# A hybrid-attention layer stack in FP32 by split products on one Trainium2 core: two chunks of the down projection as seven block products

## The chip, the cores and the metric

The kernel runs on one core of a Trainium2 chip. The metric is the device time of one execution in microseconds (us). The kernel before has a median of 1004.43 us over three runs (1003.47 to 1004.53). All inputs and the output are float32.

## The reference

The model has two layers on 256 tokens of width 1024. Each layer is a feed-forward network (ffa), a mixer (two kinds of attention) and a second feed-forward network (ffb); each adds its result to x. The change touches the feed-forward networks alone:

```python
def swiglu(x, w_gate, w_up, w_down):
    return (jax.nn.silu(x @ w_gate) * (x @ w_up)) @ w_down
...
    for l in range(DEPTH):
        x = x + 0.5 * swiglu(rms_norm(x, ffa_norm[l]), ffa_w_gate[l], ffa_w_up[l], ffa_w_down[l])
        x = x + hybrid_mixer(rms_norm(x, mix_norm[l]), w_in[l],
        ...
        x = x + 0.5 * swiglu(rms_norm(x, ffb_norm[l]), ffb_w_gate[l], ffb_w_up[l], ffb_w_down[l])
    return rms_norm(x, final_norm)
```

So four feed-forward networks run in a program. In each, w_gate and w_up are 1024 x 2816 and w_down is 2816 x 1024.

## The kernel before, in words

**Split products.** A float32 matrix is split into two float32r parts, high (`whi`, `xhi`, `hhi`) and low (`wlo`, `xlo`, `hlo`). A product of two such matrices is three matmuls, high by high, high by low and low by high, which `prod3` (L316 to L324) issues at L321, L322 and L323. For weights, ScalarE copies 128 x 1024 elements to the high part (L302) and VectorE subtracts that from the raw tile to get the low part (L281). One unit of weights is 1 MB (2048 elements on each partition) and takes two such pairs.

**A feed-forward network.** The 2816 hidden columns are five chunks of 512 and a half chunk of 256; the 256 tokens are two tiles t of 128. For chunks 0, 2, 4 and 5, gate and up are plain products. For chunks 1 and 3, gate and up together are a 2 x 2 block product (two token tiles by two halves of the input width, times those two halves by gate and up) and go by seven block products instead of eight, named 1 to 7. Four of them need sums of blocks of x on the left, which VectorE makes and which are split into the tiles named `fnhi`, `fnlo`, `fohi`, `folo`. The weights' sums are made by DMA: the tile that holds one block, when it is split, is added to in place by a second transfer from HBM (`accum_op` add, on the queue of GpSimd, L261), and is then split again. Products 1, 5, 6 and 4 share one tile in such a chain, 3 and 7 another, and 2 has its own. The result h = silu(gate) * up is turned by TensorE (L549) and split into `hhi` (L554) and `hlo` (L556).

**The down projection.** h (22 blocks k of 128 rows) is multiplied by w_down, as 11 units of two k each (`down`, from L699). Four accumulators of one PSUM bank each (token tile t by column half c, tag `acc`) collect all 22 k. One unit is 2 x 2 x 2 x 3 = 24 matmuls of 512 columns. The last two units (`TAIL`) go accumulator by accumulator, so that `close` (L720) can add 0.5 times a finished accumulator to x (L723) while the next one runs.

**What sets the order.** The program is written by generators that a small planner (`Flow`) steps in the order of its own clock and cost table, so the order of each engine's instructions is fixed when it is built. `loader` fetches the raw tiles in the order in which units are made, on the queue of SyncE (L247), with 5 raw tiles. `adder` issues the adding transfers on GpSimd's queue, in their order, each when the split before it in its chain is over. `splitter` splits the units in their order, with 6 pairs of split halves, that is, 3 units; a pair comes free when the last matmul that reads it is over. The list `PLANS` orders the products of gate and up: "g0" is the gate of chunk 0, "41" is product 4 of chunk 1.

The two lines around which the stage turns:

```python
                    prod(pd[t, c], hs, t, k, u, i, slice(c * 512, (c + 1) * 512), k == 0, k == 21)
...
            nc.vector.scalar_tensor_tensor(x[:, t, sl], pd[t, c], 0.5, x[:, t, sl],
```

Of the kernel before, what the change touches and what calls it, by code (L numbers as in the profile page):

```python
# [44 lines left out]
    "g0 u0 11 g2 51 21 31 u2 61 71 13 g4 41 53 23 33 u4 63 73 h5 43".split(),) * 3  # L45
AC = 0.1
# [86 lines left out]
def hybrid_kernel(ctx, tc, x_in, ffa_norm, ffa_w_gate, ffa_w_up, ffa_w_down, mix_norm, w_in,  # L133
# [310 lines left out]
    def ffn_units(wg, wu, wd, plan, first):  # L444
# [6 lines left out]
        def block(c, m, kh):  # L451
            return cols((wg, wu)[m], c * 512, 512, kh)
# [12 lines left out]
        for z in plan:  # L465
            kind, c = z[0], int(z[1:])
            if kind in "gu":
# [3 lines left out]
            elif kind == "h":  # L471
                for kh in range(2):
                    us[z, kh] = order([cols(wg, 2560, 256, kh), cols(wu, 2560, 256, kh)], 4, 512)
            elif kind in "1564":
                step(("x", c), c, kind, *{"1": (0, 0), "5": (1, 0), "6": (1, 1), "4": (0, 1)}[kind], kind == "4")
            elif kind in "37":
                step(("y", c), c, kind, *{"3": (1, 1), "7": (1, 0)}[kind], z == [q for q in plan if q[0] in "37" and q[1:] == z[1:]][-1])
            else:
                step(("z", c), c, kind, 0, 1, True)
        for j in range(11):  # L480
            src = wd[j * 256:(j + 1) * 256].rearrange("(i p) n -> p i n", i=2)
            us["d", j] = order(src, 2, 1024)
        return us

    def ffn(us, nm, nxt, plan, last=False):
# [8 lines left out]
        def event(*k):  # L494
            return evs.setdefault(k, Event())
# [196 lines left out]
        if inner:  # L692
            fl.spawn(factors())
            fl.spawn(sums(), 1)
        for i, z in enumerate(plan):
            if z[0] in "1234567":
# [6 lines left out]

        def down(j, t, cs, free):
            u = us["d", j]
            yield ev[j // 2, t]
            for c in cs:
                if j == 0:
                    yield fl.get("acc")
                    pd[t, c] = bank("acc", 4)  # L710
                for i in range(2):
                    k = 2 * j + i
                    yield u.when(i)
                    prod(pd[t, c], hs, t, k, u, i, slice(c * 512, (c + 1) * 512), k == 0, k == 21)
# [4 lines left out]

        def close(t, c):  # L720
            sl = slice(c * 512, (c + 1) * 512)
            yield fl.clock + HOP
            nc.vector.scalar_tensor_tensor(x[:, t, sl], pd[t, c], 0.5, x[:, t, sl],  # L723
# [6 lines left out]
        for j in range(11 - TAIL):  # L730
            for t in range(T):
                yield from down(j, t, (0, 1), t == 1)
# [3 lines left out]
        for i, (t, c) in enumerate(ends):  # L736
            for j in range(11 - TAIL, 11):
                yield from down(j, t, (c,), i == 3)
# [913 lines left out]
```

## Time and profile before

| what | us or share |
|---|---|
| median of three runs | 1004.43 |
| the profiled execution, its own time | 1003.63 |
| its span, first to last instruction | 1001.8 |
| TensorE matmul busy | 989.3 (99%) |
| TensorE weight load busy | 826.5 (82%) |
| VectorE busy | 735.1 (73%) |
| ScalarE busy | 611.0 (61%) |
| granted TensorE clock, mean | 0.998 |

The busy times are those of the profile's page; a matmul's recorded end is modelled and lies behind the start of the next, so the share of TensorE is read together with its waits. The span is 1.8 us shorter than the execution's own time. The four down projections start at 131.7, 442.2, 623.4 and 934.1 us of the span and last about 61 us each. Line numbers in the rows are those of the kernel before.

### The profile page before, as it was taken

How to read it: one execution, taken by the hardware profiler on the slowest of the kernel's cores; microseconds unless marked ns; L12 is line 12 of the kernel's file. 1: busy time of each engine (PE TensorE's matmuls, PEld its weight loads, DVE VectorE, ACT ScalarE, POOL GpSimd, SP SyncE). 2: the span in 40 equal slices, each digit the busy share in tenths (PEclk: the TensorE clock that was granted, in tenths of full speed). 3: DMA queues.
4: the chain of work that ended last, by engine and by line, in shares of the span. 5: the costliest groups of instructions: out<-in, count | busy, mean ns of one | idle time of the engine just before them, and what ended most of it. 6: DMA issues, size and time to landing. Idle time of an engine off the chain costs nothing.

```text
span 1001.8 us, 14192 instructions
## 1 busy us (share of the span) xinstructions
PE 989.3 (99%) x5268; PEld 826.5 (82%) x5268; DVE 735.1 (73%) x1365; ACT 611.0 (61%) x1061; POOL 53.6 (5%) x61
## 2 busy tenths in 40 slices
PE   9999999999999999999999999999999999999997
PEld 7877888898987888888888888888988878888885
DVE  6889854587787978784488768447878789688544
ACT  7666553558785676653367566336687766665433
POOL 1021000100000011100001110001000001110000
PEclk9999999999999999999999999999999999999999
DMA  9899965363743799975548998553645238999611
GB/s 337 260 206 303 292 236 177 103 201 111 270 137 116 194 255 278 267 266 184 195 143 225 295 270 267 195 182 114 213 171 203 91 126 222 284 262 305 229 65 42
DMA packets 100981, 207.62 MB, mean 207 GB/s; under 512 B 3784, under 2 KB 23376, under 8 KB 100912
## 3 DMA queue, kind: packets, MB, share of 16 engines
q1 hardware_dynamic: 83072, 171.65, 49.2%
q0 software_dynamic: 17536, 34.54, 19.3%
q8 instruction: 41, 0.67, 0.3%
q10 hardware_dynamic: 304, 0.53, 0.1%
q14 instruction: 28, 0.23, 0.1%
HBM read 205.66 MB, written 1.05 MB: 206 GB/s over the span
## 4 chain that ended last, share of the span: by engine, by line
PE 93%; DMA 2%; DVE 2%; issue 1%; ACT 1%; POOL 0%; POOLq 0%
PE acc L321 19%; PE acc L323 18%; PE acc L322 18%; PE sb L322 7%; PE sb L323 7%; PE sb L321 7%; DMA raw<-in_ffa_w_up_dram 2%; PE acc L338 2%; PE acc L339 2%; PE acc L340 2%; PE acc L1079 2%; PE tb L549 2%; PE tb L1059 2%; PE tb L407 1%; DVE wlo L281 1%
## 5 line engine op out<-in xcount | busy, mean ns | idle before, releaser
L281 DVE TENSOR_TENSOR wlo<-raw,whi 128x1024 fp32r<-128x1024 f32 (+2 forms) x404 | 450.2, 1136 | 169.2 <-ACT whi L302 168.7
L302 ACT ACTIVATE whi<-raw 128x1024 fp32r<-128x1024 f32 (+2 forms) x404 | 388.0, 990 | 236.8 <-PE acc L323 99.2
L321 PE MATMUL acc<-whi,hhi 128*128 128x512 f32 x352 | 138.4, 393 | 0.0
L323 PE MATMUL acc<-whi,hlo 128*128 128x512 f32 x352 | 137.2, 390 | 0.0
L322 PE MATMUL acc<-wlo,hhi 128*128 128x512 f32 x352 | 137.0, 389 | 0.0
L321 PE MATMUL acc<-whi,xhi 128*128 128x512 f32 (+1 forms) x336 | 131.9, 392 | 0.0
L322 PE MATMUL acc<-wlo,xhi 128*128 128x512 f32 (+1 forms) x336 | 128.0, 381 | 0.0
L323 PE MATMUL acc<-whi,xlo 128*128 128x512 f32 (+1 forms) x336 | 127.9, 381 | 0.0
L322 PE MATMUL sb<-wlo,xhi 128*128 128x512 f32 x304 | 118.5, 390 | 0.8 <-DVE wlo L281 0.8
L321 PE MATMUL sb<-whi,xhi 128*128 128x512 f32 x304 | 119.3, 392 | 0.0
L323 PE MATMUL sb<-whi,xlo 128*128 128x512 f32 x304 | 118.5, 390 | 0.0
L323 PEld LDWEIGHTS acc<-whi,hlo 128*128 128x128 f32 x352 | 66.1, 188 | 14.0
L322 PEld LDWEIGHTS acc<-wlo,hhi 128*128 128x128 f32 x352 | 66.1, 188 | 13.5
L321 PEld LDWEIGHTS acc<-whi,hhi 128*128 128x128 f32 x352 | 66.1, 188 | 13.2
L323 PEld LDWEIGHTS acc<-whi,xlo 128*128 128x128 f32 x336 | 63.1, 188 | 12.2
L321 PEld LDWEIGHTS acc<-whi,xhi 128*128 128x128 f32 x336 | 63.4, 189 | 11.2 <-issue 0.7
L322 PEld LDWEIGHTS acc<-wlo,xhi 128*128 128x128 f32 x336 | 63.3, 188 | 10.5
L322 PEld LDWEIGHTS sb<-wlo,xhi 128*128 128x128 f32 x304 | 57.1, 188 | 12.8 <-DVE wlo L281 1.2
L323 PEld LDWEIGHTS sb<-whi,xlo 128*128 128x128 f32 x304 | 57.1, 188 | 12.0
L321 PEld LDWEIGHTS sb<-whi,xhi 128*128 128x128 f32 x304 | 57.1, 188 | 11.6
L338 PE MATMUL acc<-xhi,whi 128*128 128x256 f32 x192 | 56.5, 294 | 0.0
L339 PE MATMUL acc<-xlo,whi 128*128 128x256 f32 x192 | 54.2, 282 | 0.0
(230 smaller groups left out, 1431.2 us busy)
## 6 DMA issues: line engine op xcount, KB each, us to landing
raw<-in_ffa_w_down_dram SPq DMA_DIRECT2D x22, 1024.0 KB, 5.0
raw<-in_ffb_w_down_dram SPq DMA_DIRECT2D x22, 1024.0 KB, 5.0
raw<-in_w_in_dram SPq DMA_DIRECT2D x20, 1024.0 KB, 5.0
raw<-in_ffb_w_gate_dram SPq DMA_DIRECT2D x20, 1024.0 KB, 5.3
raw<-in_ffa_w_gate_dram SPq DMA_DIRECT2D x18, 1024.0 KB, 8.2
raw<-in_ffa_w_up_dram SPq DMA_DIRECT2D x16, 1024.0 KB, 7.3
raw<-in_ffb_w_up_dram SPq DMA_DIRECT2D x16, 1024.0 KB, 6.6
raw<-in_ffa_w_up_dram POOLq DMA_DIRECT2D x12, 1024.0 KB, 9.7
```

The source lines that it names most:

```text
L281: nc.vector.tensor_tensor(view(u, lo, i, True), source(u, i), view(u, hi.bitcast(F32), i, True), OP.subtract)
L302: nc.scalar.activation(view(u, u.halves[-1][0], i, True), source(u, i), AF.Copy)
L321: nc.tensor.matmul(ps, xh, wh, start=first, stop=False, skip_group_check=True)
L322: nc.tensor.matmul(ps, xh, wl, start=False, stop=False, skip_group_check=True)
L323: nc.tensor.matmul(ps, xl, wh, start=False, stop=last, skip_group_check=True)
L338: nc.tensor.matmul(ps, wh, xs[0][:, k], start=first and j == 0, stop=False, skip_group_check=True)
L339: nc.tensor.matmul(ps, wh, xs[1][:, k], start=False, stop=False, skip_group_check=True)
L340: nc.tensor.matmul(ps, wl, xs[0][:, k], start=False, stop=last, skip_group_check=True)
L407: nc.tensor.transpose(ps[:, i * n + (t - ts[0]) * 128:i * n + (t - ts[0] + 1) * 128], x[:, t, k * 128:(k + 1) * 128], ident)
L549: nc.tensor.transpose(ps[:, j * 128:(j + 1) * 128], h[:, j * 128:(j + 1) * 128], ident)
L1059: nc.tensor.transpose(ps[:, j * 128:(j + 1) * 128], pp[:, i * n + s_ * 128:i * n + (s_ + 1) * 128], ident)
L1079: nc.tensor.matmul(grp.o[u * 64:(u + 1) * 64, h // 2 * 128:(h // 2 + 1) * 128], val(s_), pT[:, j * 128:(j + 1) * 128], start=u not in grp. ...
```

## The change

For the chunks 0 and 2 (k = 0 to 3 and 8 to 11), the down projection is seen as a 2 x 2 block product: two token tiles by two chunks of h, times two chunks by two column halves of w_down. It is computed by seven block products of four k each. The other seven units (p2, p3, p6 to p10) stay as they were. `DOWN` gives the order: "5d" is product 5, "p8" is the old unit 8. Products 2, 3 and 4 add straight into three of the four accumulators. Products 1, 5, 6 and 7 go into banks with the tag `sb`, are combined by VectorE with tiles that ScalarE copied (`rest_d`), and are added to x by VectorE (`add_x`) before `close` adds the accumulators. Sums of blocks of h are made by VectorE (`sums_d`), from the moment at which the last product of gate and up, 43, is next (`AHEAD`), and are split into the same four buffers as the sums of x. The weights' sums are made as in gate and up: the chain 1d, 5d, 6d, 4d in one raw tile, 3d, 7d in a second, 2d alone.

```diff
@@ -43,6 +43,8 @@
 HOP = 0.3
 PLANS = ("g0 u0 g2 11 u2 51 21 31 13 61 71 g4 41 53 23 33 u4 63 73 h5 43".split(),) + (
     "g0 u0 11 g2 51 21 31 u2 61 71 13 g4 41 53 23 33 u4 63 73 h5 43".split(),) * 3
+DOWN = "1d p2 2d p8 5d p9 3d p3 6d p6 7d 4d p7 p10".split()
+AHEAD = 1
...
@@ -449,6 +451,9 @@
         chain = {}
 
         def block(c, m, kh):
+            if c == "d":
+                r = (0, 2)[kh] * 512
+                return wd[r:r + 512, m * 512:(m + 1) * 512].rearrange("(k p) n -> p k n", p=128)
             return cols((wg, wu)[m], c * 512, 512, kh)
 
         def step(key, c, p, m, kh, end):
@@ -462,9 +467,13 @@
             us[p, c] = Unit(r, done=end)
             chain[key] = (chain[key][0], us[p, c])
 
-        for z in plan:
-            kind, c = z[0], int(z[1:])
-            if kind in "gu":
+        for z in plan + DOWN:
+            kind = z[0]
+            c = "d" if z[1] == "d" else int(z[1:])
+            if kind == "p":
+                src = wd[c * 256:(c + 1) * 256].rearrange("(i p) n -> p i n", i=2)
+                us["d", c] = order(src, 2, 1024)
+            elif kind in "gu":
                 m = "gu".index(kind)
                 for kh in range(2):
                     us[z, kh] = order(block(c, m, kh), 4, 512, loads=4 if first and z == plan[0] else 1)
@@ -474,12 +483,9 @@
...
             elif kind in "37":
-                step(("y", c), c, kind, *{"3": (1, 1), "7": (1, 0)}[kind], z == [q for q in plan if q[0] in "37" and q[1:] == z[1:]][-1])
+                step(("y", c), c, kind, *{"3": (1, 1), "7": (1, 0)}[kind], z == [q for q in plan + DOWN if q[0] in "37" and q[1:] == z[1:]][-1])
             else:
                 step(("z", c), c, kind, 0, 1, True)
-        for j in range(11):
-            src = wd[j * 256:(j + 1) * 256].rearrange("(i p) n -> p i n", i=2)
-            us["d", j] = order(src, 2, 1024)
         return us
 
     def ffn(us, nm, nxt, plan, last=False):
@@ -692,7 +698,53 @@
         if inner:
             fl.spawn(factors())
             fl.spawn(sums(), 1)
+        dforms, dk = {}, {}
+
+        def sums_d():
+            for c in (0, 2):
+                for t in range(T):
+                    yield ev[c, t]
+            blocks = []
+            for t in range(T):
+                for c in (0, 2):
+                    yield fl.get("work")
+                    a = wk([128, 512], "a")
+                    h, l = (z[:, 4 * c:4 * c + 4, t * 128:(t + 1) * 128].bitcast(F32) for z in hs)
+                    nc.vector.tensor_tensor(a.rearrange("p (k c) -> p k c", k=4), h, l, OP.add)
+                    yield fl.dve(512)
+                    blocks.append(a)
+            a11, a12, a21, a22 = blocks
+            ho, lo = ([big.tile([128, 4, 256], F32R, name="f" + z, tag=z).rearrange(
+                "p a b -> p (a b)").rearrange("p (f n) -> p f n", f=2) for z in tags]
+                for tags in (("nhi", "ohi"), ("nlo", "olo")))
+            todo = iter((("5", 0, a22), ("6", 1, a11), ("3", 2, a12), ("7", 3, a21)))
+
+            def parts(f, i, z):
+                h, l = ho[i // 2][:, i % 2], lo[i // 2][:, i % 2]
+                nc.scalar.activation(h, z, AF.Copy)
+                yield fl.act(512)
+                nc.vector.tensor_tensor(l, z, h.bitcast(F32), OP.subtract)
+                e = fl.dve(512)
+                fl.put("work", 0, e)
+                dforms[f] = [y.rearrange("p (k c) -> p k c", k=4) for y in (h, l)]
+                event("dform", f).set(e)
+
+            nc.vector.tensor_tensor(a22, a22, a21, OP.subtract)
+            yield fl.dve(512)
+            nc.vector.tensor_tensor(a21, a11, a21, OP.subtract)
+            yield fl.dve(512)
+            nc.vector.tensor_tensor(a11, a22, a11, OP.add)
+            yield fl.dve(512)
+            nc.vector.tensor_tensor(a12, a12, a11, OP.subtract)
+            yield fl.dve(512)
+            for z in todo:
+                yield from parts(*z)
+
         for i, z in enumerate(plan):
+            if i == len(plan) - AHEAD:
+                fl.spawn(sums_d(), 1)
...
@@ -701,25 +753,96 @@
             yield from last()
         pd = {}
 
+        def bank_d(t, c):
+            if (t, c) not in pd:
+                yield fl.get("acc")
+                pd[t, c] = bank("acc", 4)
+                return True
+            return False
+
         def down(j, t, cs, free):
             u = us["d", j]
             yield ev[j // 2, t]
             for c in cs:
-                if j == 0:
-                    yield fl.get("acc")
-                    pd[t, c] = bank("acc", 4)
+                new = yield from bank_d(t, c)
                 for i in range(2):
                     k = 2 * j + i
                     yield u.when(i)
-                    prod(pd[t, c], hs, t, k, u, i, slice(c * 512, (c + 1) * 512), k == 0, k == 21)
+                    prod(pd[t, c], hs, t, k, u, i, slice(c * 512, (c + 1) * 512), new and i == 0, k == 21)
                     yield
             if free:
                 free_w()
                 free_w()
 
+        def add_x(src, f, t, c):
+            xv = x[:, t, c * 512:(c + 1) * 512]
+            nc.vector.scalar_tensor_tensor(xv, src, f, xv, op0=OP.mult, op1=OP.add)
+            e = fl.dve(512)
+            event("x", t, c).set(e)
+            return e
+
+        def rest_d():
+            yield event("D1")
+            yield fl.get("p")
+            s = md([128, 512], "p", NP)
+            nc.scalar.activation(s, dk["1"], AF.Copy)
+            e = fl.act(512)
+            yield e
+            fl.put("sb", 0, e)
+            add_x(s, 0.5, 0, 0)
+            yield event("D5")
+            yield fl.get("p")
+            w = md([128, 512], "p", NP)
+            nc.scalar.activation(w, dk["5"], AF.Copy)
+            fl.put("sb", 0, fl.act(512))
+            yield event("D6")
+            nc.vector.tensor_tensor(s, s, dk["6"], OP.subtract)
+            e = fl.dve(512)
+            fl.put("sb", 0, e)
+            yield e
+            nc.vector.tensor_tensor(w, w, s, OP.add)
+            yield fl.dve(512)
+            add_x(w, -0.5, 0, 1)
+            yield event("D7")
+            nc.vector.tensor_tensor(w, w, dk["7"], OP.add)
+            yield fl.dve(512)
+            nc.vector.tensor_tensor(s, s, dk["7"], OP.add)
+            e = fl.dve(512)
+            fl.put("sb", 0, e)
+            yield e
+            fl.put("p", 0, add_x(w, -0.5, 1, 1))
+            fl.put("p", 0, add_x(s, 0.5, 1, 0))
+
+        def product_d(p):
+            u = us[p, "d"]
+            alone = {"2": (0, 0), "3": (0, 1), "4": (1, 0)}.get(p)
+            if p in "124":
+                c, t = {"1": (0, 0), "2": (2, 0), "4": (2, 1)}[p]
+                yield ev[c, t]
+                left = [z[:, 4 * c:4 * c + 4, t * 128:(t + 1) * 128] for z in hs]
+            else:
+                yield event("dform", p)
+                left = dforms[p]
+            if alone:
+                new = yield from bank_d(*alone)
+                ps = pd[alone]
+            for i in range(4):
+                yield u.when(i)
+                if i == 0 and not alone:
+                    yield fl.get("sb")
+                    ps, new = bank("sb", 2), True
+                    dk[p] = ps
+                wh, wl = u.part(i)
+                prod3(ps, left[0][:, i], left[1][:, i], wh, wl, new and i == 0, i == 3)
+                yield
+                if i % 2:
+                    free_w()
+            event("D" + p).set(fl.clock + HOP)
+
         def close(t, c):
             sl = slice(c * 512, (c + 1) * 512)
             yield fl.clock + HOP
+            yield event("x", t, c)
             nc.vector.scalar_tensor_tensor(x[:, t, sl], pd[t, c], 0.5, x[:, t, sl],
                                            op0=OP.mult, op1=OP.add)
             e = fl.dve(512)
@@ -727,15 +850,19 @@
             yield e
             nxt(t, c)
 
-        for j in range(11 - TAIL):
-            for t in range(T):
-                yield from down(j, t, (0, 1), t == 1)
+        fl.spawn(rest_d())
+        for z in DOWN[:-TAIL]:
+            if z[0] == "p":
+                for t in range(T):
+                    yield from down(int(z[1:]), t, (0, 1), t == 1)
+            else:
+                yield from product_d(z[0])
         ends = [(t, c) for t in range(T) for c in range(2)]
         if not last:
             ends = [(t, c) for c, t in ends]
         for i, (t, c) in enumerate(ends):
-            for j in range(11 - TAIL, 11):
-                yield from down(j, t, (c,), i == 3)
+            for z in DOWN[-TAIL:]:
+                yield from down(int(z[1:]), t, (c,), i == 3)
             fl.spawn(close(t, c))
 
 
```

The engines' instructions move at two places. The first is VectorE's at the beginning of the down projection of the second network. Before, from the instruction that makes chunk 3's last piece of h (L654) on; raw_4208 and raw_4240 are the units p3 and p4, raw_4259 is p5:

```order
L654 SCALAR_TENSOR_TENSOR p_4002<-p_4002,neg_3315,p_3868 128x512
L556 TENSOR_TENSOR hlo_3314<-tb_4343,hhi_3313 128x4x128
L281 TENSOR_TENSOR wlo_4353<-raw_4208,whi_4352 128x1024
L281 TENSOR_TENSOR wlo_4364<-raw_4208,whi_4363 128x1024
L281 TENSOR_TENSOR wlo_4388<-raw_4240,whi_4387 128x1024
L281 TENSOR_TENSOR wlo_4398<-raw_4240,whi_4397 128x1024
L281 TENSOR_TENSOR wlo_4422<-raw_4259,whi_4421 128x1024
```

Now, from right behind the same instruction (L654, now L660) on; raw_4262 is p8, raw_4126 is here 5d, raw_4294 is p9; a_4381, a_4357, a_4326 and a_4340 are the blocks of h for the sums, and fnlo_4409 is the low part of the sum that product 5 reads:

```order
L779 SCALAR_TENSOR_TENSOR x_78<-p_4392,x_78 128x512
L734 TENSOR_TENSOR a_4381<-a_4381,a_4357 128x512
L283 TENSOR_TENSOR wlo_4396<-raw_4262,whi_4395 128x1024
L736 TENSOR_TENSOR a_4357<-a_4326,a_4357 128x512
L283 TENSOR_TENSOR wlo_4417<-raw_4262,whi_4416 128x1024
L562 TENSOR_TENSOR hlo_3368<-tb_4428,hhi_3367 128x4x128
L738 TENSOR_TENSOR a_4326<-a_4381,a_4326 128x512
L283 TENSOR_TENSOR wlo_4444<-raw_4126,whi_4443 128x1024
L740 TENSOR_TENSOR a_4340<-a_4340,a_4326 128x512
L283 TENSOR_TENSOR wlo_4456<-raw_4126,whi_4455 128x1024
L283 TENSOR_TENSOR wlo_4472<-raw_4294,whi_4471 128x1024
L728 TENSOR_TENSOR fnlo_4409<-a_4381,fnhi_4407 128x512
```

Between the splits stand the sums; four more rows (`a` from `hhi` and `hlo`, L715) stand ahead of this piece. Over the whole program VectorE gets 104 more instructions, 26 for each network, and TensorE 48 fewer.

The second place is GpSimd's queue in the same network. Before, the last adding transfers of gate and up are followed by those of the next network; raw_3629 and raw_3861 are the chains of chunk 3:

```order
L261 DMA raw_3629<-in_ffb_w_up_dram 128x4x512 x2
L261 DMA raw_3861<-in_ffb_w_up_dram 128x4x512
L261 DMA raw_3629<-in_ffb_w_gate_dram 128x4x512
L261 DMA raw_4620<-in_ffa_w_up_dram 128x4x512 x2
L261 DMA raw_4869<-in_ffa_w_up_dram 128x4x512
```

Now four stand between them; raw_4126 is the chain of 1d, 5d, 6d and 4d, raw_4375 that of 3d and 7d:

```order
L263 DMA raw_3683<-in_ffb_w_gate_dram 128x4x512
L263 DMA raw_4126<-in_ffb_w_down_dram 128x4x512 x2
L263 DMA raw_4375<-in_ffb_w_down_dram 128x4x512
L263 DMA raw_4126<-in_ffb_w_down_dram 128x4x512
L263 DMA raw_4747<-in_ffa_w_up_dram 128x4x512 x2
```

The four are, in this order, the additions for 5d, 6d, 7d and 4d. SyncE's queue has ten plain loads of w_down for each network where it had eleven.

## Rows read from the trace of the kernel before

**Rows 1.** The page, busy time and share of the span of each engine

```profile
PE 989.3 (99%) x5268; PEld 826.5 (82%) x5268; DVE 735.1 (73%) x1365; ACT 611.0 (61%) x1061; POOL 53.6 (5%) x61
```

**Rows 2.** Who waited for whom on TensorE, whole span: us, times, longest

```profile
PE acc L322 <- DVE wlo L281: 2.7, 3, 1.1
...
PE sb L322 <- DVE wlo L281: 0.8, 1, 0.8
PE tb L407 <- DVE wlo L281: 0.3, 1, 0.3
```

**Rows 3.** TensorE in order of time, second down projection: start, us, line

```profile
451.77 0.39 PE L321 MATMUL acc<-whi,hhi 128*128 128x512 f32 x1
451.99 0.39 PE L322 MATMUL acc<-wlo,hhi 128*128 128x512 f32 x1
452.22 0.39 PE L323 MATMUL acc<-whi,hlo 128*128 128x512 f32 x1
...
454.49 0.39 PE L321 MATMUL acc<-whi,hhi 128*128 128x512 f32 x1
```

**Rows 4.** Tile hhi, second network, first matmul of three: ns, first and last start

```profile
L321 PE MATMUL acc<-whi,hhi x88: 389/389/479, 442.2 to 503.1; 128*128 128x512 f32 x88
```

**Rows 5.** Stretches, down projection, then gate and up: length, busy times, PEclk, DMA

```profile
442.20:503.50 61.30, 61.30 (x278) 50.71 (x277) 29.55 (x36) 24.69 (x35) 0.00 (x0) 1.00 0.57 189
378.00:442.20 64.20, 64.20 (x300) 53.20 (x299) 52.67 (x58) 40.70 (x48) 5.13 (x4) 1.00 0.98 274
```

**Rows 6.** ScalarE and VectorE in order of time, second down projection: splits

```profile
469.65 2.01 ACT L302 ACTIVATE whi<-raw 128x1024 fp32r<-128x1024 f32 x2 [3.43 <-PE acc L323]
...
470.74 2.36 DVE L281 TENSOR_TENSOR wlo<-raw,whi 128x1024 fp32r<-128x1024 f32 x2 [3.08 <-ACT whi L302]
```

**Rows 7.** Groups by line and shape, VectorE, then ScalarE: count, busy us, mean ns

```profile
L281 DVE TENSOR_TENSOR wlo<-raw,whi 128x1024 fp32r<-128x1024 f32 x340 | 407.3, 1220 | 165.2 <-ACT whi L302 165.0
L556 DVE TENSOR_TENSOR hlo<-tb,hhi 128x512 fp32r<-128x512 f32 x40 | 27.4, 686 | 11.5 <-ACT hhi L554 11.0
L515 DVE TENSOR_TENSOR p<-xhi,xlo 128x512 f32<-128x512 f32 x16 | 10.9, 684 | 0.0
L654 DVE SCALAR_TENSOR_TENSOR p<-p,neg 128x512 f32<-128x512 f32 x8 | 6.0, 745 | 0.0
L584 DVE SCALAR_TENSOR_TENSOR sg<-sb,rs,sg 128x256 f32<-128x256 f32 x8 | 3.8, 481 | 0.9 <-ACT sg L539 0.9
L556 DVE TENSOR_TENSOR hlo<-tb,hhi 128x256 fp32r<-128x256 f32 x8 | 3.3, 416 | 0.0
...
L302 ACT ACTIVATE whi<-raw 128x1024 fp32r<-128x1024 f32 x340 | 349.5, 1057 | 222.6 <-PE acc L323 99.2 <-PE sb L323 43.3 <-issue 25.8
L554 ACT ACTIVATE hhi<-tb 128x512 fp32r<-128x512 f32 x40 | 23.7, 593 | 35.0 <-PE tb L549 33.1 <-issue 1.9
```

**Rows 8.** VectorE in order of time, around the start of the second down projection

```profile
432.25 3.56 DVE L281 TENSOR_TENSOR wlo<-raw,whi 128x1024 fp32r<-128x1024 f32 x3
...
437.79 1.23 DVE L281 TENSOR_TENSOR wlo<-raw,whi 128x1024 fp32r<-128x1024 f32 x1 [1.38 <-ACT whi L302]
439.24 0.48 DVE L584 SCALAR_TENSOR_TENSOR sg<-sb,rs,sg 128x256 f32<-128x256 f32 x1 [0.23 <-ACT sg L539]
440.51 1.23 DVE L281 TENSOR_TENSOR wlo<-raw,whi 128x1024 fp32r<-128x1024 f32 x1 [0.78 <-ACT whi L302]
```

**Rows 9.** Line L261, the adding transfers: issue ns on GpSimd, then us to landing

```profile
L261 POOL DMA_DIRECT2D raw<-in_ffb_w_up_dram x12: 1273/1282/1328, 341.2 to 897.5; - x12
...
DMA to landing us min/median/max: 8.4/9.7/14.9
```

**Rows 10.** DMA issues by line: count, KB, median us from issue to landing

```profile
raw<-in_ffa_w_down_dram SPq DMA_DIRECT2D x22, 1024.0 KB, 5.0
...
raw<-in_ffb_w_up_dram POOLq DMA_DIRECT2D x12, 1024.0 KB, 9.4
...
raw<-in_ffb_w_gate_dram POOLq DMA_DIRECT2D x4, 1024.0 KB, 13.6
```

## The prediction, made before the changed kernel ran

> **What bounds the kernel now.** I read the page first: TensorE's matmuls are busy 99% of the span, VectorE 73%, ScalarE 61% [rows 1]. A matmul's recorded end lies behind the next one's start, so that share alone proves little. The second view is what TensorE waited for: in the whole span it waited 2.7 + 0.8 + 0.3 = 3.8 us for split weights [rows 2]. The third is its order of time inside a down projection: the first and the thirteenth of a run of matmuls start at 451.77 and 454.49, so twelve take 2.72 us and one 0.2267 us [rows 3]; the recorded 0.39 us overlap. The granted clock is 1.00 there and in gate and up, the 2.4 GHz level [rows 5]. So TensorE issues at an even pace, and time goes with the count of matmuls, as long as its operands come.
>
> The stretches say how far they are from coming late. In the down projection VectorE works 29.55 of 61.30 us and ScalarE 24.69; in gate and up VectorE works 52.67 of 64.20 (82%), with the DMA engines at 0.98 [rows 5]. In the down projection, each split waits for matmuls to free its pair of halves ("PE acc L323") and ends 3.45 us later, at 473.10 [rows 6]: the weights stand ready early.
>
> **What is removed.** The order counts 48 matmuls fewer, so the change does what it says: of the 4 x 3 x 88 = 1056 (88 of each kind in one network [rows 4]), 96 for each network become 84. They have the same shape, so 48 x 0.2267 = 10.9 us go from the engine that sets the end. The result banks, their tags and the left sides change, but a matmul from the sums' tiles is no slower in gate and up than any other, so I give that nothing.
>
> **What is added, for each network.**
> - VectorE: 3 more units to split, 6 x 1.22; sums of h, 4 + 4 + 4 at 0.684; results, 4 at 0.69 and 4 into x at 0.745 [rows 7]. That is 7.3 + 8.2 + 5.7 = 21.2 us on 29.55, or 51 of some 58.5 us: 87%. Gate and up run at 82% without a wait of TensorE in the later networks. Costed at nothing, if it comes in time (below); with no cover it would be 21 us.
> - ScalarE: 6 x 1.057, and 6 copies at 0.593 = 9.9 us [rows 7], on 24.69. 60%, hidden.
> - Four adding transfers on GpSimd's queue, 8.4 to 14.9 us from issue to landing, and 10 plain loads instead of 11, 5.0 us each [rows 9, 10]. The chain's tile is held longer, so three raw tiles are left for the other units; by the 3-unit rule of the splitter their loads still land over 8 us ahead. GpSimd issues nothing else here but, in the last network, the final gains.
> - `close` now also waits for `add_x`. The last two additions stand behind product 7, and the first accumulator that needs one is finished 36 matmuls, 8.2 us, later. Costed at nothing.
>
> **Does VectorE come in time at the start?** I count from the first down matmul (442.2 in the second network [rows 4]). Product 5 is the first to read a sum; ahead of it stand 72 matmuls, so it is due at 72 x 0.2267 = 16.3. In the new order VectorE has from p2's first split (437.79, that is, -4.4 [rows 8]) to the low part that product 5 reads 26 instructions: 9 splits, 9 of the kind of 0.684, one evacuation and one piece of h at 0.69, two at 0.745, two at 0.481, two at 0.416. Full durations make 21.8 us. But neighbours overlap: three splits took 3.56, not 3.66, and the splits of [rows 6] 2.36 for two, so some 0.08 us less for each, 19.7 us. The window is 4.4 + 16.3 = 20.7. So it comes 1.0 early by the one and 1.1 late by the other, and 2.1 late with the idle 0.23 + 0.78 that VectorE shows in this piece before [rows 8]. I take the overlapped value, as rows of this very engine show it, and that the idle gaps are filled: other work now stands in the queue. Bounds: 0 and 2.1 us for each network.
>
> **Does the chain of additions come in time?** 1d is split where p0 was (435.81 [rows 8]), so 5d's transfer has 15 us. 5d is split by about 13.6, from the same count. 6d's addition, at the typical 9.4 [rows 10], lands at 23.0; its pair is free only at 24.5 (108 matmuls), so its split ends at 28.0. 4d's addition lands at 37.4, its split ends at 40.8, and 4d is due at 192 x 0.2267 = 43.5: 2.7 us to spare. At 8.4 it is more. At 13.6, the median of the last addition of the chain in gate and up [rows 10], it is 13.6 + 13.6 + 3.45 + 13.6 + 3.45 = 47.7, so 4.2 us late. I take 9.4: in the down projection the DMA engines are at 0.57, not 0.98 [rows 5], and loads land in 5.0 us. Bounds: 0 and 4.2.
>
> **Sum.** 1003.63 of the profiled execution - 10.9 = 992.7. For first uses that come a little late I add 0.5, less than the 3.8 us that gate and up's eight chains and everything else show [rows 2]: 993.2. The profiled execution lies 0.8 under the median of the three runs and inside their spread; halfway between, I say 993.5 us.
>
> **A rule against it, port of GpSimd.** What the row shows: an addition takes 1273 to 1328 ns to issue, whatever VectorE does beside it [rows 9], and that within stretches in which VectorE is busy 82% [rows 5]. The Trainium skill, SBUF — State Buffer, Who interferes with whom, says that a VectorE instruction in a two-port mode locks GpSimd out, so that the descriptors of its transfers wait. By that rule more VectorE work would mean later additions; the skill excepts tensor_tensor from that mode, and the rows agree with the exception. By the rule without it, an issue would wait for one instruction, 1.22 us, and 4d would still land in time (break-even is worked out below).
>
> **Rivals.**
> - *VectorE is late at the start.* 1.1 to 2.1 us for each network, 4.4 to 8.4 in all: 997.1 to 1001.1. For it: the count above is within a microsecond. Against: gate and up do the same sums amid splits with no wait. Near the end, p10's second split has some 0.4 us left as well, behind the two results of product 7. Chance 0.15.
> - *The chain is late, and the kernel slower.* Place: 4d's addition. Without loss while two landings take under 23.0 us, that is, 11.5 each; the gain of a network, 2.72 us, is gone at 12.85 each. At 13.6, 4.2 x 4 = 16.8 us: 1009.5. Behind 4d, p7 and p10 wait in the same splitter. For it: 13.6 and 14.9 are there. Against: they fell beside two or three loads in flight; here there is one. Chance 0.06.
> - *TensorE isn't the bound.* If matmuls only filled time that operands set, fewer would change nothing: 1003.6. Against: no wait in these stretches, and a steady 0.2267. The Trainium skill, Perfetto Trace Analysis, Identifying the Most-Contended Engine, says that matmul busy time is no measure and weight loads are; these are busy 82% [rows 1], so by that rule 18% would be slack, and this rival would hold. I give it 0.04, since the starts are even.
>
> **How the numbers follow.** Forecast 0.73 (992 to 996), VectorE late 0.15, chain late 0.06, no change 0.04, and 0.02 for a stall that I have not seen. About 0.2%, 2 us, can be told from no change here. Faster: 0.73 + 0.15, and a little of the chain's case at under 12.85, makes 0.89. Same: 0.05. Slower: 0.06. The range goes from 991.8 (the lowest run, 1003.47, less 10.9, and 0.8 for the spread) to 999.5, which takes in most of the first rival.
>
> **What would show it.** Right: matmuls in the banks of the down projections down by 48, the starts still 0.227 apart, a down projection from first to last matmul some 2.7 us shorter, TensorE's waits for split weights and sums under 5 us in all, VectorE at about 87% in that stretch. The first rival shows as waits of product 5 (left sides `fnhi`, `fnlo`) for VectorE at 16 us into each stretch, or of p10 near its end. The second shows as ScalarE waiting for a w_down transfer ahead of 4d, landings of 12 us or more, and TensorE waiting for `wlo` near 43 us. The third shows as a span unchanged with more waiting. I am wrong if fewer matmuls leave the stretches as long as they were.

## The result, and the profile after

The changed kernel takes 998.21 us, median of 4 runs (997.24 to 1000.67); the kernel before, in the same comparison, 1004.48 (4 runs, 1003.47 to 1005.22). The ratio is 0.9942, 95% interval 0.9922 to 0.9962: faster by 6.3 us. The prediction was 993.5, within 991.8 to 999.5: direction and range hold, but of the 10.9 us that it removed 4.6 us came back. The profiled execution is the fastest of the four, 997.24 us, with a span of 995.5.

The page after: busy time by engine, and from its third part the two DMA queues that move nearly all bytes (packets, MB, share of 16 engines' span).

```profile
PE 979.6 (98%) x5220; PEld 817.1 (82%) x5220; DVE 807.6 (81%) x1469; ACT 647.2 (65%) x1109; POOL 74.3 (7%) x77
...
q1 hardware_dynamic: 85056, 167.46, 47.8%
q0 software_dynamic: 25984, 51.32, 29.1%
```

The same two lines of the page before, which the rows ahead of the prediction did not include:

```profile
q1 hardware_dynamic: 83072, 171.65, 49.2%
q0 software_dynamic: 17536, 34.54, 19.3%
```

Against [rows 1], TensorE has 48 matmuls fewer, as counted. VectorE has 104 instructions more, 26 for each network as counted, and 72.5 us more, 18.1 for each (21.2 predicted); ScalarE 48 more and 36.2 us, 9.0 for each (9.9 predicted). The adding transfers run on q0, the plain loads on q1. Per MB a queue's share times the span gives, on q0, 0.291 x 995.5 / 51.32 = 5.6 us of all 16 engines, and on q1 0.478 x 995.5 / 167.46 = 2.8. Before it was the same: 0.193 x 1001.8 / 34.54 = 5.6, and 2.9. So **an addition of 1.05 MB takes 5.9 us of the 16 engines' packet time, a load of the same size 3.0**, and the page before already said so. The packet times of two queues can overlap, so this is not time in which the engines do nothing else.

What TensorE waited for, whole span (us, times, longest), after:

```profile
PE acc L324 <- DVE wlo L283: 6.3, 8, 1.1
PE acc L1728 <- POOL ident masks.py:199: 1.4, 1, 1.4
PE sb L324 <- DVE wlo L283: 0.8, 1, 0.8
PE tb L555 <- DVE sg L580: 0.3, 1, 0.3
```

Waits for split weights have grown from 2.7 + 0.8 [rows 2] to 6.3 + 0.8, by 3.6 us and five waits. One of the five, 0.62 us at 72.39, is in the first network's gate and up, ahead of any down projection. The other four, 3.0 us, are at p10 in the first three networks' down projections; of p10's two low parts the second comes late in each network, in the third the first as well. TensorE in order of time (start, us, line, operation, then idle time and what ended it):

```profile
182.59 0.50 PE L324 MATMUL acc<-wlo,hhi 128*128 128x512 f32 x1 [0.76 <-DVE wlo L283]
...
491.70 0.50 PE L324 MATMUL acc<-wlo,hhi 128*128 128x512 f32 x1 [0.77 <-DVE wlo L283]
492.04 0.40 PE L325 MATMUL acc<-whi,hlo 128*128 128x512 f32 x1
492.27 0.39 PE L323 MATMUL acc<-whi,hhi 128*128 128x512 f32 x1
492.50 0.40 PE L324 MATMUL acc<-wlo,hhi 128*128 128x512 f32 x1
...
670.44 0.50 PE L324 MATMUL acc<-wlo,hhi 128*128 128x512 f32 x1 [0.66 <-DVE wlo L283]
...
672.17 0.50 PE L324 MATMUL acc<-wlo,hhi 128*128 128x512 f32 x1 [0.77 <-DVE wlo L283]
```

The starts otherwise stay 0.23 apart, as in [rows 3]. At the four waits they are 1.16, 1.17, 1.04 and 1.16 apart: 0.93 + 0.94 + 0.81 + 0.93 = 3.6 us lost. The fourth network has none.

**Where a wait comes from**, in the second network, whose first down matmul starts at 441.2. GpSimd's issues of the last three additions, then ScalarE and VectorE in order of time:

```profile
455.05 1.28 POOL L263 DMA_DIRECT2D raw<-in_ffb_w_down_dram  x1 [18.59 <-DVE wlo L283]
462.28 1.28 POOL L263 DMA_DIRECT2D raw<-in_ffb_w_down_dram  x1 [5.94 <-DVE wlo L283]
469.79 1.28 POOL L263 DMA_DIRECT2D raw<-in_ffb_w_down_dram  x1 [6.23 <-DVE wlo L283]
```

```profile
481.85 2.01 ACT L304 ACTIVATE whi<-raw 128x1024 fp32r<-128x1024 f32 x2 [5.36 <-DMA raw<-in_ffb_w_down_dram]
```

```profile
482.94 1.23 DVE L283 TENSOR_TENSOR wlo<-raw,whi 128x1024 fp32r<-128x1024 f32 x1 [3.68 <-ACT whi L304]
484.09 0.68 DVE L779 SCALAR_TENSOR_TENSOR x<-p,x 128x512 f32<-128x512 f32 x1
484.69 3.49 DVE L283 TENSOR_TENSOR wlo<-raw,whi 128x1024 fp32r<-128x1024 f32 x3
488.10 0.68 DVE L807 TENSOR_TENSOR p<-p,sb 128x512 f32<-128x512 f32 x1
488.69 1.22 DVE L283 TENSOR_TENSOR wlo<-raw,whi 128x1024 fp32r<-128x1024 f32 x1
489.83 0.68 DVE L809 TENSOR_TENSOR p<-p,sb 128x512 f32<-128x512 f32 x1
490.43 1.22 DVE L283 TENSOR_TENSOR wlo<-raw,whi 128x1024 fp32r<-128x1024 f32 x1
```

The additions of 6d, 7d and 4d are issued 7.2 and 7.5 us apart; matched with their landings they take 9.87, 12.10 and 11.96 us. ScalarE is idle for 5.36 us until the last lands at 481.75. From 482.94 on VectorE has no pause: the splits of 4d, p7 and p10 stand in a row, and between them one addition to x and product 7's two results (L807, L809). The last split ends at 491.65, and TensorE goes on at 491.70. So it takes two things together: 4d's addition lands late, and VectorE has other work among the six splits behind it.

By stretches (length, then busy us of TensorE, its weight loads, VectorE, ScalarE, GpSimd, then PEclk, DMA share, GB/s), the down projections of the second and the last network:

```profile
441.20:501.60 60.40, 59.63 (x270) 48.70 (x270) 47.10 (x61) 33.30 (x47) 3.85 (x3) 1.00 0.86 250
...
930.70:988.30 57.60, 57.60 (x258) 47.62 (x257) 46.18 (x60) 32.52 (x42) 3.91 (x3) 1.00 0.62 162
```

The DMA share in the second network has risen from 0.57 [rows 5] to 0.86, from 34.9 to 51.9 us. Three additions for one plain load would be 3 x 5.9 - 3.0 = 14.7 of these 17. In the last network no weights of a next part are loaded beside them, the share is 0.62, and 4d lands after 9.71 us. There VectorE also has less between the splits: product 7's second result (L809, at 978.18) stands behind both splits of p10.

### The profile page after: what moved, and what is told of

It reads as the page before. It is cut to its first block, busy times and chain, and to the rows that moved or that the text cites. A ratio compares the mean times of both kernels' runs of the same rounds, so it can differ in the third digit from the quotient of the medians.

```text
span 995.5 us, 14306 instructions
## 1 busy us (share of the span) xinstructions
PE 979.6 (98%) x5220; PEld 817.1 (82%) x5220; DVE 807.6 (81%) x1469; ACT 647.2 (65%) x1109; POOL 74.3 (7%) x77
## 3 DMA queue, kind: packets, MB, share of 16 engines
q1 hardware_dynamic: 85056, 167.46, 47.8%
q0 software_dynamic: 25984, 51.32, 29.1%
HBM read 218.24 MB, written 1.05 MB: 220 GB/s over the span
## 4 chain that ended last, share of the span: by engine, by line
PE 81%; DMA 8%; DVE 6%; issue 3%; ACT 1%; POOL 0%; POOLq 0%; ACTq 0%; DVEq 0%
PE acc L324 14%; PE acc L323 14%; PE acc L325 14%; PE sb L324 7%; PE sb L325 7%; PE sb L323 7%; DMA raw<-in_ffa_w_down_dram 4%; DVE wlo L283 4%; DMA raw<-in_ffa_w_up_dram 3%; PE acc L340 2%; PE acc L341 2%; PE acc L342 2%; PE acc L1206 2%; PE tb L1186 2%; PE tb L555 2%
## 5 line engine op out<-in xcount | busy, mean ns | idle before, releaser
L283 DVE TENSOR_TENSOR wlo<-raw,whi 128x1024 fp32r<-128x1024 f32 (+2 forms) x428 | 478.4, 1139 | 112.7 <-ACT whi L304 112.2
L304 ACT ACTIVATE whi<-raw 128x1024 fp32r<-128x1024 f32 (+2 forms) x428 | 412.1, 993 | 191.1 <-PE sb L325 44.5
L324 PE MATMUL acc<-wlo,hhi 128*128 128x512 f32 x256 | 100.3, 392 | 3.0 <-DVE wlo L283 3.0
L323 PE MATMUL acc<-whi,hhi 128*128 128x512 f32 x256 | 100.9, 394 | 0.0
L325 PE MATMUL acc<-whi,hlo 128*128 128x512 f32 x256 | 99.9, 390 | 0.0
L324 PEld LDWEIGHTS acc<-wlo,xhi 128*128 128x128 f32 x336 | 63.2, 188 | 10.7
L324 PEld LDWEIGHTS acc<-wlo,hhi 128*128 128x128 f32 x256 | 48.1, 188 | 14.7 <-DVE wlo L283 5.2
L325 PEld LDWEIGHTS acc<-whi,hlo 128*128 128x128 f32 x256 | 48.1, 188 | 9.9
L323 PEld LDWEIGHTS acc<-whi,hhi 128*128 128x128 f32 x256 | 48.1, 188 | 9.7
L342 PE MATMUL acc<-xhi,wlo 128*128 128x256 f32 x192 | 54.2, 282 | 0.0
```

Source lines behind the costliest of these rows:

```text
L283: nc.vector.tensor_tensor(view(u, lo, i, True), source(u, i), view(u, hi.bitcast(F32), i, True), OP.subtract)
L304: nc.scalar.activation(view(u, u.halves[-1][0], i, True), source(u, i), AF.Copy)
L323: nc.tensor.matmul(ps, xh, wh, start=first, stop=False, skip_group_check=True)
L324: nc.tensor.matmul(ps, xh, wl, start=False, stop=False, skip_group_check=True)
L325: nc.tensor.matmul(ps, xl, wh, start=False, stop=last, skip_group_check=True)
L342: nc.tensor.matmul(ps, wl, xs[0][:, k], start=False, stop=last, skip_group_check=True)
```

## The experiments

Ratios are to the kernel before in the same comparison: 1003.99 us (7 runs) for the first four, 1004.44 (7 runs) for the last three.

**Product 7's results later.** One line in the task that takes the products' results, behind its wait for product 7, holds the two results back for some microseconds of the planner's clock; in the order of VectorE they come behind p10's splits. Behind p10, the planner also puts some matmuls, transposes and splits in another order than in the changed kernel.

```diff
             yield event("D7")
+            yield fl.clock + 4.0
             nc.vector.tensor_tensor(w, w, dk["7"], OP.add)
```

> The part of rest_d behind product 7 waits 4 us more in the planner, so that the two VectorE instructions which read product 7's bank (L807, L809 in the changed kernel) stand behind both splits of p10 in VectorE's order instead of around them. Theory (chain late and splits in a row): from the landing of 4d's addition on, VectorE works without a pause up to p10's second split, so 1.2 us of other work taken out of that row ends the 0.9 us wait of TensorE at p10 in the first three networks: TensorE's waits for split weights fall from 7.1 us to 4.4 or less, the time by 2 to 3.6 us, to about 995.5. Landing of 4d's addition stays at 11.8 to 12 us. Rival (the additions alone set it, what stands between the splits is beside the point): waits stay at 7 us and the time at 998.

Measured: 995.07 us (994.33 to 996.64), ratio 0.9912 (0.9897 to 0.9926). 4d's addition still lands late (12.21 us in the second network), but VectorE now runs its splits without the results between:

```profile
484.85 0.69 DVE L779 SCALAR_TENSOR_TENSOR x<-p,x 128x512 f32<-128x512 f32 x1
485.45 6.90 DVE L283 TENSOR_TENSOR wlo<-raw,whi 128x1024 fp32r<-128x1024 f32 x6
492.26 0.68 DVE L808 TENSOR_TENSOR p<-p,sb 128x512 f32<-128x512 f32 x1
```

TensorE's starts before p10's second half are 0.56 and 0.44 apart in the first two networks instead of 1.16 and 1.17; in the others there is no gap. So taking 1.2 us of other work from between the splits gives back 3.1 of the 3.6 us at p10, with the landing about as late. The medians say 3 us as well, though the 95% intervals of the two ratios just overlap (0.9897 to 0.9926 here, 0.9922 to 0.9962 for the changed kernel).

**4d without its addition.** 4d is loaded plainly and not added to the chain's tile; the sum is left out for this unit, everything behind it is the same work.

```diff
+            if c == "d" and p == "4":
+                us[p, c] = order(src, 4, 512)
+                chain[key][1].done = True
+                return
```

> The weights of product 4d come by a plain load into a raw tile of their own; the addition of the other three blocks to them is left out (so is what it would add to the result). VectorE's and ScalarE's counts and order stay. Theory (4d's late addition): 4d is split as soon as its pair is free, the waits at p10 and 4d in the down projections are gone, TensorE's waits for split weights fall from 7.1 us to about 3.5, as in the kernel before, and the time to about 994.5, near the 993.5 of the sum. Rival (VectorE is too full in this stretch, whatever the landing): p10 still waits some 0.9 us for each network, and the time stays at 998.

Measured: 993.50 us (992.39 to 993.65), ratio 0.9891 (0.9877 to 0.9906). TensorE's waits for weights are down to 3.5 + 0.8 us (2.7 + 0.8 before; what is more is nearly all one wait of 0.74 us in the first network's gate and up), and no gap is left in a down projection:

```profile
PE acc L324 <- DVE wlo L283: 3.5, 4, 1.1
...
PE sb L324 <- DVE wlo L283: 0.8, 1, 0.8
PE tb L559 <- DVE sg L584: 0.5, 1, 0.5
```

So what is left of the change is worth 1003.99 - 993.50 = 10.5 us: 10.9 for 48 matmuls, less about half a microsecond.

**7d without its addition.** The same four lines with `p == "7"`; 4d's addition stays, 7d's is left out.

> The weights of product 7d come by a plain load into a raw tile of their own; the addition of 3d's block to them is left out (so is what it would add to the result). Theory (three additions in a row share the DMA engines): with one of them replaced by a plain load, 4d's addition lands 9.5 to 10.5 us after its issue instead of 11.8 to 12.0, p10's wait is gone, and the time is about 994.5 to 995.5. Rival (each addition is slowed by the plain loads beside it, not by the other additions): 4d's landing stays at 11.5 or more, the wait stays, and the time is 998.

Measured: 993.75 us (992.26 to 994.12), ratio 0.9893 (0.9876 to 0.9909). With no addition just ahead of it, 4d's now takes 9.80, 9.89, 9.48 and 8.56 us to land, and no gap is left. The DMA view of this kernel, 441 to 495 us (line, queue, operation, KB, median us to landing):

```profile
raw<-in_ffb_w_down_dram SPq DMA_DIRECT2D x5, 1024.0 KB, 6.0
...
raw<-in_ffb_w_down_dram POOLq DMA_DIRECT2D x2, 1024.0 KB, 9.6
```

The same view of the changed kernel:

```profile
raw<-in_ffb_w_down_dram SPq DMA_DIRECT2D x5, 1024.0 KB, 6.8
raw<-in_ffb_w_down_dram POOLq DMA_DIRECT2D x3, 1024.0 KB, 12.0
raw<-in_ffa_w_gate_dram SPq DMA_DIRECT2D x3, 1024.0 KB, 8.0
```

So 4d's 12 us are not those of an addition as such: with one addition less in that stretch it lands 2 us sooner. That does not decide between the two sides of the expectation: while 4d was in flight, the plain loads also moved less than in the changed kernel, 1.08 MB instead of 2.03 (table further on).

**Additions further apart.** 6d and 7d each one unit earlier in the order.

```diff
-DOWN = "1d p2 2d p8 5d p9 3d p3 6d p6 7d 4d p7 p10".split()
+DOWN = "1d p2 2d p8 5d p9 3d 6d p3 7d p6 4d p7 p10".split()
```

> 6d goes ahead of p3 and 7d ahead of p6: 1d p2 2d p8 5d p9 3d 6d p3 7d p6 4d p7 p10. Nothing else is changed. 6d's split is over some 5 us earlier for the same place of 4d, so 4d's addition has 5 us more. Theory (4d's addition is late by place, not by nature): 4d lands before its pair is free, p10's wait is gone, and the time is about 994.5 to 995.5; but 6d now is due at 27.2 us into the stretch and its addition lands at about 24, so a wait of 0 to 1 us there for each network is possible, which would give 995 to 998.5. Rival (VectorE too full): waits move but stay near 7 us, and the time is 998.

Measured: 996.64 us (994.55 to 997.40), ratio 0.9922 (0.9907 to 0.9937). Here 7d's addition, still issued 7.2 us behind 6d's, lands after 9.02 us in the second network instead of 12.10, and 4d's after 11.70, 10.58, 10.64 and 10.80: the distance of two additions alone does not make one late; 7d met 0.94 MB of plain loads here and 1.96 in the changed kernel. Starts 1.16 apart at p10 have become ones of 0.47 to 0.59 in the first, third and fourth networks, with none in the second. Alone, the intervals of this kernel and of the changed one overlap, so it is not shown to be better.

**The chain spread out from its start.** 5d moved ahead of 2d, 6d ahead of 3d, 4d ahead of 7d; the task that forms the sums of h is started one unit of the plan earlier (`AHEAD`); and a delay of 3, at the place of the first experiment.

```diff
-DOWN = "1d p2 2d p8 5d p9 3d p3 6d p6 7d 4d p7 p10".split()
-AHEAD = 1
+DOWN = "1d p2 5d p8 2d p9 6d p3 3d p6 4d 7d p7 p10".split()
+AHEAD = 2
...
             yield event("D7")
+            yield fl.clock + 3.0
```

> The same computation in another order, 1d p2 5d p8 2d p9 6d p3 3d p6 4d 7d p7 p10, with the sums of h begun one unit earlier (AHEAD 2) and the two results of product 7 put 3 us later. The four additions now come some 13, 14 and 8 us apart instead of 20, 7 and 7.5, so none should overlap another for long. Theory (three additions in a row on GpSimd's queue hold up 4d): 4d's and 7d's additions land 8.5 to 10 us after their issue, well before their pairs are free, the waits at p10 and 4d are gone, and the time is 993 to 994.5, as in the runs with one addition left out. What may go wrong: 5d is now due 8.2 us into the stretch, and the sums must be ready by then; if they are not, a wait of 1 to 2 us at 5d for each network gives 998 to 1001. Rival (any four additions in this stretch cost some 4 us): 998.

Measured: 1010.77 us (1009.20 to 1012.42), ratio 1.0063 (1.0048 to 1.0078): slower than before the change. TensorE's waits in this kernel, and in order of time two in the second network at product 5, whose left side is `fnhi`:

```profile
PE sb L324 <- DVE wlo L283: 6.2, 11, 0.8
PE acc L324 <- DVE wlo L283: 4.6, 12, 1.1
```

```profile
454.60 0.50 PE L324 MATMUL sb<-wlo,fnhi 128*128 128x512 f32 x1 [0.66 <-DVE wlo L283]
...
456.94 0.50 PE L324 MATMUL sb<-wlo,fnhi 128*128 128x512 f32 x1 [0.68 <-DVE wlo L283]
```

The first down matmul starts at 444.5 here. 1d's split ends 3.3 us before it, where it ended 6.3 before in the changed kernel; 5d's addition, issued at 441.76, lands at 452.15 and is split late for product 5, which TensorE now reaches at 453.54. At the end 4d's addition takes 11.26 us and 7d's, behind it, 14.04. The first three networks pay near product 5 and again at products 7 and p10, the last near product 5 alone. So this way of spreading takes from the chain's start what it gives to its end, and a chain with too little room does end on the slower side, as the prediction's second rival has it, at other places than the one it names and beyond the 998 to 1001 us that the expectation gave for this case. Over TensorE's whole order, the distances of more than 0.36 us between two starts add up, less 0.2267 each, to 21.5 us here and to 10.8 in the changed kernel; these 10.7 are most of the 12.8 by which the two profiled executions differ. The rest was not followed further, nor which of the three edits costs most.

**Both remedies.** The order of the fourth experiment and the delay of the first.

```diff
-DOWN = "1d p2 2d p8 5d p9 3d p3 6d p6 7d 4d p7 p10".split()
+DOWN = "1d p2 2d p8 5d p9 3d 6d p3 7d p6 4d p7 p10".split()
...
             yield event("D7")
+            yield fl.clock + 4.0
```

> The order with 6d ahead of p3 and 7d ahead of p6, and the two results of product 7 put 4 us later. In the run with that order alone 4d's addition landed earlier, but the time was 996.6, while its profiled execution, with waits of 4.2 us for split weights, took 994.55. Theory (what was left was the row of VectorE's work near p10, met in some executions only): 994.5 to 995.5. Rival (in that order 6d and 7d wait for their additions in some executions): unchanged, 996.5.

Measured: 994.26 us (993.22 to 995.36), ratio 0.9899 (0.9884 to 0.9914). This is the lowest median of the whole computation, below the changed kernel in the same comparison by 3.5 us (the intervals are apart) and within a microsecond of the two runs that leave an addition out. The intervals of this run and of either remedy alone overlap, so it is not shown that two do more than one. 4d lands 38.5 us after the first down matmul of the second network instead of 40.5, and the four splits of 4d and p7 run ahead of the results of product 7. Those results and, behind p10's first split, two additions to x (L779, 486.33 to 487.62) still stand ahead of p10's second split, as they do in the order without the delay:

```profile
479.45 4.63 DVE L283 TENSOR_TENSOR wlo<-raw,whi 128x1024 fp32r<-128x1024 f32 x4 [2.04 <-ACT whi L304]
484.00 0.68 DVE L808 TENSOR_TENSOR p<-p,sb 128x512 f32<-128x512 f32 x1
484.60 0.68 DVE L810 TENSOR_TENSOR p<-p,sb 128x512 f32<-128x512 f32 x1
485.19 1.22 DVE L283 TENSOR_TENSOR wlo<-raw,whi 128x1024 fp32r<-128x1024 f32 x1
```

Two small gaps are left in its down projections, 0.25 us in the first network and 0.46 in the third. What the delay adds to the order is therefore open.

**The changed kernel again.**

> The changed kernel as it is, beside the two others on the same chip. Expected: 998.2 within 1 us; waits of TensorE for split weights near 7 us, at p10 of the first three networks and once at 4d; no wait at 5d.

Measured: 997.80 us (996.55 to 1000.44), ratio 0.9940 (0.9921 to 0.9959). The waits stand in the same places: late starts at p10 of the first three networks, 4d landing after 11.95, 12.84 and 11.77 us there and 9.23 in the last, none at product 5. There is none at 4d either, in this execution or the first, where the expectation had one.

## Why the prediction was right, and where it was off

- **The bound and what is removed: right.** TensorE issues at an even 0.23 us, and 48 matmuls fewer are worth their 10.9 us: the two kernels without the late wait lie 10.5 and 10.2 us below the kernel before, at 993.50 and 993.75 where the sum said 993.5. The third rival, that matmuls only fill time, falls with that. The Trainium skill (Perfetto Trace Analysis, Identifying the Most-Contended Engine) names two measures for TensorE, the share of peak arithmetic and the busy share of weight loads; the prediction took the second alone. By it, at 82% before and after, 18% would have been slack; here the time followed the count of matmuls and not that share.
- **VectorE at the start: right to a tenth of a microsecond, with a deadline that was 0.8 us too early.** The low part of the left side that product 5 reads was foreseen at 15.3 us after the first matmul (16.3 less 1.0). It ends at 456.49, that is, 15.2; TensorE reads it first at 458.81. 5d's split ends at 13.5, foreseen 13.6. Product 5 was foreseen at 16.3 and starts at 17.1, since six transposes stand ahead of it in TensorE's order that the count of 72 matmuls leaves out; 4d starts at 44.3 for the same reason, not 43.5. So the first rival shows no wait at product 5. The place that it adds, "p10's second split has some 0.4 us left as well, behind the two results of product 7", is where the waits are; but there it needed the next point as well.
- **The share of VectorE: a little off.** 47.10 of 60.40 us is 78%, not 87%: the durations of its 59 instructions in that stretch add up to 50.9 us, as foreseen (51), but neighbours overlap by some 0.06 us, which the sum of full durations ignores. The time did not hang on it.
- **The chain: the step that failed.** The text took 9.4 us for a landing, since "in the down projection the DMA engines are at 0.57, not 0.98". 6d went as foreseen: landing at 23.7 us (23.0), split done at 28.2 (28.0). Then 4d's addition took 11.96 us, and 4d landed at 40.5, not 37.4, 3.1 us late and more than the 2.7 us to spare. The 0.57 was the share before the change, and the change itself raised it to 0.86: an addition takes 5.9 us of packet time, three of them were issued within 15 us, and plain loads ran beside them. The price lay in the page before, as a queue's share of time beside its MB; the prediction priced landings, and not what the transfers take from each other. It also set aside the landings of 13.6 us and more because "they fell beside two or three loads in flight; here there is one". There were three: p7's load, issued at 464.28, and two of the next network's gate weights, issued at 471.79 and 477.96. Its bounds of 0 and 4.2 us for each network did hold the loss: 0.93, 0.94, 1.74 and nothing.
- **The point from which lateness costs: 2 us too far.** The second rival said "without loss while two landings take under 23.0 us", and counted to 4d alone. 6d's and 4d's landings add up to 21.98, 21.83, 23.57 and 20.06 us in the four networks. In the first two networks the sum is under 23.0 and some 0.9 us is lost all the same, at p10: "Behind 4d, p7 and p10 wait in the same splitter" was written there without a price. By these rows the loss begins somewhere between 20.06 and 21.83. The two landings taken, 18.8, kept clear of that; slower, at 12.85 each, was not reached.
- **The range: held in part by luck.** 998.21 lies outside the forecast's 992 to 996 and inside the range because its upper end, 999.5, was set for VectorE coming late at the start, which did not happen. That the time falls among that rival's 997.1 to 1001.1 us is chance as well: these were worked out from lateness at the start, and p10, which the rival also names, had no price of its own. What made p10 late was the chain, and its rival had 0.06. Of the prediction's own signs of being right, waits under 5 us (7.1 measured), VectorE at 87% and a down projection 2.7 us shorter failed: the first three networks' are 1.1, 1.0 and 0.3 us shorter from first to last matmul, and only the last is 2.7. Of the second rival's signs, ScalarE waited for w_down transfers ahead of 4d and landings came to 12 us, but TensorE waited from some 49 us on, at p10, and not near 43.
- **The port of GpSimd: as the rows said.** The issues in the down projections take 1273 to 1341 ns after the change [rows 9 for before], with VectorE at 78% beside them. That agrees with the exception that the Trainium skill (SBUF — State Buffer, Who interferes with whom) makes for tensor_tensor. Over the whole program one issue, for ffa's up weights, takes 1826 ns, before and after alike; the 1273 to 1328 ns that the prediction reads from [rows 9] are those of one group. The additions are late between issue and landing, not at the issue:

```profile
L263 POOL DMA_DIRECT2D raw<-in_ffb_w_down_dram x8: 1273/1282/1341, 435.2 to 959.2; - x8
...
DMA to landing us min/median/max: 8.4/10.0/14.3
```

How do 4d's 12 us divide between the additions ahead of it and the plain loads beside it? The traces tell which bytes the two queues moved while an addition was in flight, from its issue to its landing (packets, MB, share). For 4d in the second network, first in the changed kernel, then with 7d loaded plainly:

```profile
q0 software_dynamic: 697, 1.36, 61.6%
q1 hardware_dynamic: 850, 2.03, 46.3%
```

```profile
q0 software_dynamic: 528, 1.05, 65.1%
q1 hardware_dynamic: 449, 1.08, 29.5%
```

The first two shares add up to 108%, which is the overlap named above. The same view for these two and six more flights; 1.05 MB of q0 are the addition's own:

| addition, kernel, network | us to landing | MB on q0 | MB on q1 |
|---|---|---|---|
| 4d, changed, second | 11.96 | 1.36 | 2.03 |
| 7d, changed, second | 12.10 | 1.47 | 1.96 |
| 4d, changed again, second | 12.84 | 1.41 | 2.30 |
| 7d, 4d loaded plainly, second | 12.82 | 1.23 | 2.72 |
| 4d, additions further apart, second | 10.58 | 1.47 | 1.09 |
| 4d, 7d loaded plainly, second | 9.89 | 1.05 | 1.08 |
| 4d, changed, last | 9.71 | 1.43 | 0.69 |
| 7d, additions further apart, second | 9.02 | 1.29 | 0.94 |

The four late ones met 1.96 to 2.72 MB of plain loads, the other four 0.69 to 1.09, while other additions' bytes are much alike in both groups. So the plain loads beside it go with most of the lateness. That is read from what happened together; a run that holds back only those loads was not tried, so their part is not shown by itself.

## What to carry to other kernels

When a change adds transfers, price them from the queue's share of time and its MB in the page, and add that to the stretch's DMA share before choosing a landing time: the share before the change is not the one that the new transfers will meet. Count the loads that will be in flight beside the last link too, those of the next part among them. For a chain of transfers, carry the count on to the last unit that stands behind its end in the same queues, with the unhurried work that stands between; here moving 1.2 us of such VectorE work gave back 3.1 of the 3.6 us lost at p10. Spreading the chain out, which here took room from its start, made the kernel slower than before the change.

## What the runs showed of the hardware

By its queue's share, an adding transfer of 1.05 MB takes 5.9 us of the 16 DMA engines' packet time, a plain load 3.0, in both kernels alike. The addition for 4d took between 8.6 us to land (last network, 7d loaded plainly) and 12.8 (second network, changed kernel again), and the later landings went with more bytes of plain loads beside them. The plain loads of w_down went from 5.0 us [rows 10] to a median of 6.8 in the second network's down projection.
